# Gate tiles read and squared inside the projection loop, and buffers of their own for low parts, modulation and out tiles

## The chip, the cores and the metric

The kernel runs on one core of a Trainium2 chip. The metric is device time in microseconds: the median of the runs of one program. TensorE multiplies, VectorE and ScalarE do elementwise work, GpSimd (POOL) starts some DMAs and sums over partitions, SyncE (SP) starts most loads.

## The reference, cut to what matters

Two transformer layers over 256 tokens of width 2048, with a second stream of 256 context tokens. Layer 0 mixes by a Fourier transform, layer 1 by attention. The change lies in layer 0:

```python
shift, scale, gate = split(silu(c) @ ada_w[i] + ada_b[i], 3)      # modulation
h = rmsnorm(x, norm_g[i]) * (1 + scale) + shift
u, z = split(h @ w_in, 2)                                         # 4096 columns each
f = fft2(u, over tokens and in groups of 256).real                # 16 groups
f = einsum('bngc,gcd->bngd', f, w_mix)
y = f * silu(z)
x = x + gate * (y @ w_out[i])
```

The context stream goes through the same with its own modulation.

## The kernel before, in words

Every matmul in float32 is done as three cheaper ones, on a rounded high part and a low part of each operand (`mm3`: high by high, high by low, low by high). In the projection the parts are float32r (`split`: a ScalarE cast, line 66, then a VectorE subtraction, line 67). In the gate and out projections they are float16 with one scale for each weight tile. That scale comes from the tile's sum of squares: `squares` (a ScalarE activation, line 161, with a sum by row), `total` (line 165, POOL, over partitions), `scale` (VectorE, lines 170 and 171, and a ScalarE copy, line 173, where a second factor is folded in), and then `split16` (ScalarE line 179, VectorE line 180).

Layer 0 runs in these stages:

1. An opening: input loads, the first modulation vectors, the token transform.
2. The projection loop over 16 groups `g`. Each group loads two 1 MB weight halves `wu` into `rawp` (three buffers, tile name `raw`), folds them into m and p parts (line 134 and 140 on VectorE, or an accumulating DMA on POOL, line 143), splits them, and runs an m part and a p part of 48 matmuls each. `load_m` prepares a small matrix of the group (its cast is tile `mh`). `mix` multiplies the group before by its matrix and sends the result to DRAM (`fd`). `evacs[g]` are the cast and the subtraction that empty the p part of group g. The 16 tiles of gate columns 0 to 511 come as four shared tiles `wz0`; in groups 8 to 11 each is loaded into `raw` and squared there, for one common scale.
3. The gate loop. `make_hs` builds the 16 h tiles again in float16 (a load of xT by POOL, then VectorE line 768, ScalarE line 769, VectorE line 770). The four shared tiles are loaded again, split in halves, and multiplied into four outputs. Then come 28 private tiles `wz`, one for each output block b from 4 to 31, each 48 matmuls.
4. The out loop over 32 tiles `wo0` (n from 0 to 31).

`fetch(n)` loads tile n of stages 3 and 4, squares it and computes its scale; `weights(n)` splits it and calls `fetch(n + 2)`. `raw6` gives the tiles of wz, wo0 and adw in turn a buffer of `rawp` and one of `zp` (three each). `adw` are the 64 tiles of the remaining modulation weights: an `ada_step` takes one of them, and VectorE multiplies and reduces it with the condition rows in `cb` (line 730). Both halves of a split, high and low, come from `wsp` (six buffers).

The instructions of an engine run in a fixed order. That order is made when the program is built, by a planner that goes by the order of the program text and its own estimate of when operands are ready. `issue_after(x)` keeps the instructions of a block, on the engine of x, behind x; it adds no wait.

At the end of stage 4, `row_sums` adds squares by matmul for the next norm, and `x1_turn` transposes the stream for layer 1.

Of the kernel before, what the change touches and what calls it, by code (L numbers as in the profile page):

```python
# [32 lines left out]
def tile_dit(ctx: ExitStack, tc: tile.TileContext, a: dict, out: bass.AP):  # L33
# [21 lines left out]
    def act(dt=F32, n=512):  # L55
        return actp.tile([P, n], dt, tag="act", name="act")
# [512 lines left out]
        fill_pe(len(fill))  # L569


    w4 = adap.tile([P, 4], F32, name="w4")
    hsc = adap.tile([P, 2, KT, 2], F32, name="hsc")
    hq = [small("hq") for _ in range(3)]
    squares(hsc[:, 0], gs0, hq[0], 64.0)
    squares(hsc[:, 1], sh0, hq[1], 1.5)
    V.tensor_tensor(hq[2], hq[0], hq[1], op=ALU.add)
    hup, hdn = scale(total(hq[2]), None, "h", 1)
    V.tensor_scalar(hsc[:, 0], gs0, hup, None, op0=ALU.mult)
    V.tensor_scalar(hsc[:, 1], sh0, hup, None, op0=ALU.mult)  # L580
# [11 lines left out]
    for g in range(G):  # L592
# [33 lines left out]
            pqh, pql, sp = m1  # L626
        elif g > 2:
            pqh, pql, sp = load_m(g)
        if g == 13:
            w1 = small("w1", bufs=1)  # L630
            V.tensor_reduce(w1, w4, axis=AX.X, op=ALU.add)
            u4, d4 = scale(total(w1), hdn, "4", 1)
# [7 lines left out]
        if g > 3:  # L640
            with after_evac(g - 1), tc.issue_after(m_end[0]), tc.issue_after(m_end[1]):
                w[1]["p"] = split_part("p", v)
        oa = {} if g > 2 else ou[g]

        def part(xs, ks=range(KT)):
# [32 lines left out]
        pl = up.tile([127, 2, 130], F32R, tag="apl", name="apl")  # L678
        split(ph, pl, oa["p"])
        evacs.append((last_cast[0], last_sub[0]))  # L680

        def mix(g=g, mh=mh, ml=ml, ph=ph, pl=pl, pqh=pqh, pql=pql, sp=sp):
            for db in range(2):
# [32 lines left out]
    def ada_jobs():  # L716
        for pieces in ((0,), (1, 2, 3)):
            for kh in range(2):
                cb = adap.tile([P, 2, 1024], F32, tag="cb", name="cb")
                with tc.issue_after(hs_end[2]):  # L720
                    nc.gpsimd.dma_start(cb, a["crow"][:, kh].broadcast_to([P, 2, 1024]))
                with tc.issue_after(hs_end[1]):
                    S.activation(cb, cb, AF.Silu)  # L723
                for i in pieces:
                    for fg in range(8):
                        w = ada_raw(a["adw"][i, kh, fg])
                        for f in range(2):
                            wf = w[:, f * 1024 : f * 1024 + 1024]
                            for s in range(2 if i < 3 else 1):
                                V.tensor_tensor_reduce(junk, wf, cb[:, s], 1.0, 0.0, ALU.mult, ALU.add, acc[:, i, kh, fg * 2 + f, s : s + 1])  # L730
# [7 lines left out]


    adat = lay0.enter_context(tc.tile_pool(name="adat", bufs=1))  # L740
    junk = adat.tile([P, 1056], BF16, name="junk")[:, 0:1024]
    acc = adat.tile([P, 4, 2, KT, 2], F32, name="acc")
    YA = 8
    with tc.tile_pool(name="yp", reuse_waits="tile", bufs=33 - YA) as ypool, tc.tile_pool(name="zp", reuse_waits="tile", bufs=3) as zp:
        ys = [act() if b < YA else ypool.tile([P, 512], F32, tag="y", name="y") for b in range(NB)]
        hs = []
        hs_end = [None] * 3
        turn = [0]

        def raw6(src, view=lambda t, s: ((t, s),)):  # L750
            turn[0] += 1
            pool, nm = (rawp, "raw") if turn[0] % 2 else (zp, "rawz")
            t = pool.tile([P, D], F32, tag=nm, name=nm)
            for d, s in view(t, src):
                last_dma[0] = nc.sync.dma_start(d, s).ins
            return t

        ada_raw = raw6

        def make_hs(k):  # L760
            xt = act()
# [8 lines left out]
                hs_end[0] = V.scalar_tensor_tensor(l, t, hsc[:, 1, k, s : s + 1], h, op0=ALU.add, op1=ALU.subtract).ins  # L770
            hs.append((hl[:, 0:512], hl[:, 512:1024]))

        yq = adap.tile([P, NB], F32, name="yq")
        yup, ydn, yy = [None] * 2, [None] * 2, []

        def z_out(b, o, dn):
# [25 lines left out]
        def fetch(n):  # L802
            if n >= len(jobs):
                return
            nm, at_, i = jobs[n]
            if nm == "wz":
                t = raw6(a["wz"][at_])
            else:
                v = a["wo0"][at_[0] // 8, i * 8 : i * 8 + 8].rearrange("g p (j b f) -> p g j b f", j=2, b=8)[:, :, :, at_[0] % 8]
                t = raw6(v, lambda t, s: [(t.rearrange("p (g j f) -> p g j f", g=8, j=2)[:, :, j], s[:, :, j]) for j in range(2)])  # L810
            h, q = half16(), small("wq")
            squares(h, t, q)
            ready[n] = t, h, *scale(total(q), hdn if nm == "wz" else ydn[i])

        def weights(n):
            t, wh, up_, dn = ready.pop(n)
            wl = half16()
            split16(wh, wl, t, up_)
            fetch(n + 2)
            return wh, wl, dn  # L820

        o4 = [psum() for _ in range(4)]
        for kg in range(4):
            wr = raw6(a["wz0"][kg])
            wh, wl = half16(), half16()
            for i in range(2):
                make_hs(kg * 4 + i * 2)
                q = slice(i * 1024, (i + 1) * 1024)
                with tc.issue_after(hs_end[0]) if kg else nullcontext(), tc.issue_after(hs_end[1]) if kg else nullcontext():
                    split16(wh[:, q], wl[:, q], wr[:, q], u4)  # L830
                make_hs(kg * 4 + i * 2 + 1)
            for j in range(4):
                k = kg * 4 + j
                for b in range(4):
                    q = slice(j * 512 + b * P, j * 512 + (b + 1) * P)
                    mm3(o4[b], wh[:, q], wl[:, q], hs[k][0], hs[k][1], k == 0, k == KT - 1)
        for b in range(4):
            with tc.issue_after(last_dma[0]):
                nc.sync.dma_start(ys[b], fd[b])
        for b in range(4):  # L840
            z_out(b, o4[b], d4)
        fetch(0)
        fetch(1)
        for b in range(4, NB):
            wh, wl, dn = weights(b - 4)
            with tc.issue_after(last_dma[0]):
                nc.sync.dma_start(ys[b], fd[b])
# [12 lines left out]
        x1, sqs, xin = [], [], {}  # L860
        sq_end, st_end, sums = [None], [None], []

        def evac0(b, i, o, dn):
            t = xin[b]
            gd = adap.tile([P, 2], F32, tag="gd", name="gd", bufs=4)
            V.tensor_scalar(gd, gt0[:, b, :], dn, None, op0=ALU.mult)
            t2 = act() if i else None
            for s in range(2):
                q = slice(s * N, (s + 1) * N)
                V.scalar_tensor_tensor(t[:, q], o[:, q], gd[:, s : s + 1], t[:, q], op0=ALU.mult, op1=ALU.add)  # L870
                if i and b >= 14:
                    sq_end[0] = S.activation(t2[:, q], t[:, q], AF.Square).ins
# [16 lines left out]
        for n, (b, i) in enumerate(outs):  # L889
            if n == 0:  # L890
                y_scale(1)
            wh, wl, dn = weights(n + NB - 4)
            if n < 4:
                for _ in range(4):
# [21 lines left out]
    x1d = dram.tile([2, P, D], F32, name="x1d")  # L916
    gated = dram.tile([1, D], F32, name="gated")

    def x1_turn(tb, c):
# [4 lines left out]
        S.copy(t, o)  # L924
# [11 lines left out]
    with tc.issue_after(st_end[0]):  # L936
# [6 lines left out]
        for c, tb in ((0, 0), (0, 1), (1, 0), (1, 1), (2, 0)):  # L943
            x1_turn(tb, c)
    r_ps = [psum()[:, 0:N] for _ in range(2)]
    for t in range(4):
# [591 lines left out]
```

## Time and profile before

| what | value |
|---|---|
| median of 3 runs | 1791.06 us (1789.63 to 1796.57) |
| profiled execution, its own time | 1785.5 us |
| its span, first to last instruction | 1783.7 us |
| mean granted TensorE clock | 0.995 |
| projection, groups 8 to 15 | about 205 to 332 us |
| gate and out loops | about 333 to 1012 us |
| HBM read | 356.26 MB |

Rows of the profile name an engine, a line of the kernel, an operation and the tiles it writes and reads (`raw<-raw`). A number in brackets behind a row is the time for which the engine stood idle before it, with what ended that wait. A row of the waits has total microseconds, count and the longest.

### The profile page before, as it was taken

To read this page: it belongs to the slowest core of one execution; us is meant where nothing else is said; L and a number is where in the kernel's file an instruction comes from. 1 tells how busy PE (TensorE), PEld (TensorE's weight loads), DVE (VectorE), ACT (ScalarE), POOL (GpSimd) and SP (SyncE) were. 2 spreads that over 40 slices of the span, in tenths; PEclk is the share of its full clock that TensorE was granted. 3 is DMA by queue.
4 is the path that set the end of the run, shared out by engine and by line. 5 is a ranking of instruction groups with operands and counts; after the bars stand their busy time and mean duration, and the time that the engine had idled before them with its cause. 6 is when DMAs were issued, how large, how long until landed. Compare 5 with 4: busy or idle time off the path is not lost. (4 is left out here: it accounts for less than half of the span.)

```text
span 1783.7 us, 25965 instructions
## 1 busy us (share of the span) xinstructions
PE 1731.1 (97%) x9449; PEld 1204.6 (68%) x9449; DVE 1398.2 (78%) x2415; ACT 1039.3 (58%) x1708; POOL 256.6 (14%) x277
## 2 busy tenths in 40 slices
PE   6999999999999999999999999999999999999997
PEld 4679999644444444444444588788888888887886
DVE  5779778789889997953587463989999999997455
ACT  5544544485565656444334343777888888887343
POOL 0002111211000001100101000322212212234001
PEclk9999999999999999999999999999999999999999
DMA  9998898857777798654468323578898988888554
GB/s 393 417 340 230 234 279 237 288 214 283 275 261 264 259 327 256 204 164 130 131 226 275 112 97 104 174 179 219 213 208 211 216 208 208 210 216 262 197 179 142
DMA packets 267777, 403.06 MB, mean 226 GB/s; under 512 B 152641, under 2 KB 218577, under 8 KB 236161
## 3 DMA queue, kind: packets, MB, share of 16 engines
q1 hardware_dynamic: 243584, 363.39, 64.9%
q0 software_dynamic: 19920, 31.06, 6.9%
q10 hardware_dynamic: 4144, 6.95, 1.2%
q8 instruction: 74, 1.21, 0.3%
q14 instruction: 55, 0.44, 0.1%
HBM read 356.26 MB, written 12.59 MB: 207 GB/s over the span
## 5 line engine op out<-in xcount | busy, mean ns | idle before, releaser
L67 DVE TENSOR_TENSOR wl<-raw,wh 128x1024 fp32r<-128x1024 f32 x205 | 272.3, 1334 | 112.0 <-ACT wh L66 109.3
L66 ACT CAST wh<-raw 128x1024 fp32r<-128x1024 f32 x205 | 214.2, 1046 | 136.9 <-PE ps L80 123.6
L730 DVE CUSTOM_DVE_ANT_0 junk<-rawz,cb 128x1024 bf16<-128x1024 f32 x200 | 244.0, 1220 | 8.5 <-ACT cb L723 5.6
L80 PE MATMUL ps<-act,w 128*128 128x512 f16 x640 | 243.5, 381 | 0.5 <-DVE act L770 0.5
L79 PE MATMUL ps<-act,w 128*128 128x512 f16 x640 | 239.4, 381 | 4.0 <-ACT w L179 2.2
L81 PE MATMUL ps<-act,w 128*128 128x512 f16 x640 | 239.6, 379 | 0.2 <-DVE w L180 0.2
L1203 PE MATMUL ps<-h,wh 128*128 128x512 f32 x512 | 187.1, 403 | 0.0
L81 PEld LDWEIGHTS <-w 128*128 128x128 f16 x1024 | 100.2, 98 | 127.9 <-DVE w L180 6.8
L79 PEld LDWEIGHTS <-w 128*128 128x128 f16 x1024 | 100.4, 98 | 125.2 <-ACT w L179 3.3
L80 PEld LDWEIGHTS <-w 128*128 128x128 f16 x1024 | 100.4, 98 | 120.6 <-issue 0.8
L180 DVE SCALAR_TENSOR_TENSOR w<-raw,up,w 128x2048 f16<-128x2048 f32 (+1 forms) x58 | 131.8, 2274 | 51.5 <-PE ps L80 45.1
L161 ACT ACTIVATE w<-raw 128x2048 f16<-128x2048 f32 x54 | 102.8, 1904 | 94.2 <-PE ps L81 50.0
L81 PE MATMUL ps<-y,w 128*128 128x512 f16 x384 | 145.2, 379 | 4.0 <-DVE w L180 4.0
L80 PE MATMUL ps<-y,w 128*128 128x512 f16 x384 | 145.4, 379 | 0.0
L79 PE MATMUL ps<-y,w 128*128 128x512 f16 x384 | 144.9, 379 | 0.0
L1205 PE MATMUL ps<-h,wl 128*128 128x256 f32 x512 | 138.4, 281 | 0.0
L179 ACT ACTIVATE w<-raw,up 128x2048 f16<-128x2048 f32 (+1 forms) x58 | 112.1, 1935 | 23.3 <-DVE up L170 22.2
L80 PE MATMUL ps<-wl,h 128*128 128x512 f32 x320 | 125.1, 391 | 0.3 <-DVE wl L67 0.3
L81 PE MATMUL ps<-wh,h 128*128 128x512 f32 x320 | 123.8, 390 | 0.0
L79 PE MATMUL ps<-wh,h 128*128 128x512 f32 x320 | 122.4, 397 | 0.0
L165 POOL PARTITION_ALL_REDUCE tot<-wq x60 | 42.6, 713 | 541.5 <-ACT w L161 456.8
L1257 DVE SCALAR_TENSOR_TENSOR f<-p,sm,f 128x512 f16<-128x512 f32 x128 | 103.1, 824 | 12.0 <-ACT f L1256 11.8
(380 smaller groups left out, 4051.7 us busy)
## 6 DMA issues: line engine op xcount, KB each, us to landing
raw<-in_wz SPq DMA_DIRECT2D x65, 1024.0 KB, 5.3
rawz<-in_adw SPq DMA_DIRECT2D x56, 1024.0 KB, 5.1
raw<-in_awp SPq DMA_DIRECT2D x32, 1024.0 KB, 12.8
raw<-in_wq SPq DMA_DIRECT2D x32, 1024.0 KB, 5.2
raw<-in_wu SPq DMA_DIRECT2D x32, 1016.0 KB, 7.3
raw<-in_wo SPq DMA_DIRECT2D x54, 512.0 KB, 5.7
raw<-in_wo1b SPq DMA_DIRECT2D x16, 1024.0 KB, 4.9
act<-in_xT POOLq DMA_DIRECT2D x32, 256.0 KB, 6.3
```

Source lines behind the costliest of these rows:

```text
L66: last_cast[0] = S.copy(h, src).ins
L67: last_sub[0] = eng.tensor_tensor(l, src, h.bitcast(F32), op=ALU.subtract).ins
L79: PE.matmul(o, wh, xh, start=start, stop=False)
L80: PE.matmul(o, wh, xl, start=False, stop=False)
L81: return PE.matmul(o, wl, xh, start=False, stop=stop).ins
L161: sq_ins[0] = S.activation(dump, src, AF.Square, scale=scale, accum_out=col).ins
L179: last_cast[0] = S.activation(h, src, AF.Copy, scale=up).ins
L180: last_sub[0] = V.scalar_tensor_tensor(l, src, up, h, op0=ALU.mult, op1=ALU.subtract).ins
L730: V.tensor_tensor_reduce(junk, wf, cb[:, s], 1.0, 0.0, ALU.mult, ALU.add, acc[:, i, kh, fg * 2 + f, s : s + 1])
L1203: PE.matmul(o[0], wh[:, q], hx1[k], start=k == 0, stop=k == KT - 1)
L1205: PE.matmul(o[0][:, 0:N], wl[:, q], hx1[k][:, 0:N], start=False, stop=False)
L1257: V.scalar_tensor_tensor(f[:, 512:1024], pt[tb], sm[:, tb : tb + 1], f[:, 0:512], op0=ALU.mult, op1=ALU.subtract)
```

## The change

- The scale of the h tiles (`hsc`) is computed in groups 6 and 7 of the projection loop, not ahead of it.
- Six tiles, the four `wz0` and the first two `wz`, are read by `read_ahead` in groups 4, 6, ... 14 into the buffer `cb`, and squared there in two halves by `square_ahead` a group later. The scales of the first two private tiles are then known, and `fetch` only loads these.
- `adw` tiles have two `zp` buffers (`rawz`) to themselves; `wz` and `wo0` tiles use only the three of `raw`. Low parts have two buffers of their own (`wl`). One more y tile lies in the `act` pool (`YA`), one fewer in `yp`; `load_y` takes it when needed.
- The gate of layer 0 is multiplied by the scale of y once (`gty`), so `wo0` tiles need no ScalarE copy in `scale`.
- Steps of the modulation are dealt out otherwise: 31 instead of 28 in the gate loop, none in the first four tiles of the out loop, two at a time in tiles 5 to 8 and 25 to 28.
- Some orders are set anew (`wp_end`, `shared_end`), and one transposition goes ahead of the last row sums.

The diff, cut to its core:

```diff
+    def read_ahead(j):
+        src = a["wz0"][j] if j < 4 else a["wz"][j - 4]
+        ahead[0] = adap.tile([P, D], F32, tag="cb", name="cb")
+        nc.sync.dma_start(ahead[0], src)
+
+    def square_ahead(j):
+        for i in range(2):
+            t = ahead[0][:, i * 1024 : (i + 1) * 1024]
+            squares(t, t, w6[:, j * 2 + i : j * 2 + i + 1])
+
+    def scale_ahead(j, n, tag):
+        w1 = small("w1", bufs=3)
+        V.tensor_reduce(w1, w6[:, j * 2 : (j + n) * 2], axis=AX.X, op=ALU.add)
+        return total(w1), tag
...
-        if 8 <= g < 12:
-            t = raw(a["wz0"][g - 8])
-            squares(t, t, w4[:, g - 8 : g - 7])
...
+        if g in (4, 6, 8, 10, 12, 14):
+            with after_evac(g - 1):
+                read_ahead(g // 2 - 2)
+        elif g > 4:
+            with after_evac(g):
+                square_ahead(g // 2 - 2)
...
-        def raw6(src, view=lambda t, s: ((t, s),)):
-            turn[0] += 1
-            pool, nm = (rawp, "raw") if turn[0] % 2 else (zp, "rawz")
...
+        def ada_raw(src):
+            t = zp.tile([P, D], F32, tag="rawz", name="rawz", bufs=2)
+            nc.sync.dma_start(t, src)
+            return t
...
-            h, q = half16(), small("wq")
+            t = raw(a["wz"][at_]) if nm == "wz" else raw_wo(*at_)
+            h = half16()
+            if n < 2:
+                ready[n] = t, h, *first[n]
+                return
+            q = small("wq")
             squares(h, t, q)
-            ready[n] = t, h, *scale(total(q), hdn if nm == "wz" else ydn[i])
+            ready[n] = t, h, *scale(total(q), hdn if nm == "wz" else None)
...
-            wl = half16()
+            wl = zp.tile([P, D], F16, tag="wl", name="wl", bufs=2)
...
-            wr = raw6(a["wz0"][kg])
+            wr = raw(a["wz0"][kg])
...
-                with tc.issue_after(hs_end[0]) if kg else nullcontext(), tc.issue_after(hs_end[1]) if kg else nullcontext():
+                with tc.issue_after(hs_end[0] if kg else wp_end[1]), tc.issue_after(hs_end[1] if kg else wp_end[0]):
                     split16(wh[:, q], wl[:, q], wr[:, q], u4)
...
-            wh, wl, dn = weights(b - 4)
+            with tc.issue_after(shared_end[0]), tc.issue_after(shared_end[1]), tc.issue_after(hs_end[1]):
+                wh, wl, dn = weights(b - 4)
...
-                ada_step(1)
+                ada_step(2 if b in (7, 10, 13) else 1)
...
-            V.tensor_scalar(gd, gt0[:, b, :], dn, None, op0=ALU.mult)
+            V.tensor_scalar(gd, gty[i][:, b, :], dn, None, op0=ALU.mult)
...
-            ada_step(0 if n > 29 else 2 if n > 19 else 1)
+            ada_step(0 if n < 4 or n > 28 else 2 if 4 < n < 9 or n > 24 else 1)
...
-    row_sums(3)
+    with tc.issue_after(e), tc.issue_after(sq_end[0]):
+        x1_turn(0, 0)
+    with tc.issue_after(turn_end[0]):
+        row_sums(3)
```

More of the change, by code (lines that the diff above doesn't have):

```diff
@@ L569, in tile_dit @@
         fill_pe(len(fill))
-    w4 = adap.tile([P, 4], F32, name="w4")
+    w6 = adap.tile([P, 12], F32, name="w6")
     hsc = adap.tile([P, 2, KT, 2], F32, name="hsc")
[L574 to L580, printed above, removed]
+    ahead, early = [None], {}
+    def read_ahead(j):
[10 more added lines that the diff above has]
+        return total(w1), tag
     fd = [dram.tile([P, 512], F32, name=f"fd{b}") for b in range(NB)]
@@ L680, in tile_dit @@
         evacs.append((last_cast[0], last_sub[0]))
+        if g in (4, 6, 8, 10, 12, 14):
[4 more added lines that the diff above has]
+                square_ahead(g // 2 - 2)
+        if g in (6, 13, 15):
+            with after_evac(g):
+                if g == 6:
+                    hq = [small("hq") for _ in range(3)]
+                    squares(hsc[:, 0], gs0, hq[0], 64.0)
+                    squares(hsc[:, 1], sh0, hq[1], 1.5)
+                    V.tensor_tensor(hq[2], hq[0], hq[1], op=ALU.add)
+                    toth = total(hq[2])
+                else:
+                    early[g] = scale_ahead(*((0, 4, "4") if g == 13 else (4, 1, "5")))
+        if g in (7, 14):
+            with after_evac(g):
+                if g == 7:
+                    hup, hdn = scale(toth, None, "h", 1)
+                    V.tensor_scalar(hsc[:, 0], gs0, hup, None, op0=ALU.mult)
+                    V.tensor_scalar(hsc[:, 1], sh0, hup, None, op0=ALU.mult)
+                else:
+                    u4, d4 = scale(early[13][0], hdn, "4", 1)
         def mix(g=g, mh=mh, ml=ml, ph=ph, pl=pl, pqh=pqh, pql=pql, sp=sp):
@@ L740, in tile_dit, with load_y, raw_wo @@
     adat = lay0.enter_context(tc.tile_pool(name="adat", bufs=1))
-    junk = adat.tile([P, 1056], BF16, name="junk")[:, 0:1024]
+    junk = adat.tile([P, 1072], BF16, name="junk")[:, 0:1024]
     acc = adat.tile([P, 4, 2, KT, 2], F32, name="acc")
-    YA = 8
-    with tc.tile_pool(name="yp", reuse_waits="tile", bufs=33 - YA) as ypool, tc.tile_pool(name="zp", reuse_waits="tile", bufs=3) as zp:
-        ys = [act() if b < YA else ypool.tile([P, 512], F32, tag="y", name="y") for b in range(NB)]
+    YA = 9
+    with tc.tile_pool(name="yp", reuse_waits="tile", bufs=33 - YA) as ypool, tc.tile_pool(name="zp", reuse_waits="tile", bufs=2) as zp:
+        ys = []
+        def load_y(b):
+            ys.append(act() if b < YA else ypool.tile([P, 512], F32, tag="y", name="y"))
+            with tc.issue_after(last_dma[0]):
+                nc.sync.dma_start(ys[b], fd[b])
         hs = []
         hs_end = [None] * 3
-        turn = [0]
-        def raw6(src, view=lambda t, s: ((t, s),)):
-            turn[0] += 1
-            pool, nm = (rawp, "raw") if turn[0] % 2 else (zp, "rawz")
-            t = pool.tile([P, D], F32, tag=nm, name=nm)
-            for d, s in view(t, src):
-                last_dma[0] = nc.sync.dma_start(d, s).ins
-            return t
-        ada_raw = raw6
+        def raw_wo(b, i):
+            t = rawp.tile([P, D], F32, tag="raw", name="raw")
+            v = a["wo0"][b // 8, i * 8 : i * 8 + 8].rearrange("g p (j b f) -> p g j b f", j=2, b=8)
+            for j in range(2):
+                last_dma[0] = nc.sync.dma_start(t.rearrange("p (g j f) -> p g j f", g=8, j=2)[:, :, j], v[:, :, j, b % 8]).ins
+            return t
+        def ada_raw(src):
+            t = zp.tile([P, D], F32, tag="rawz", name="rawz", bufs=2)
+            nc.sync.dma_start(t, src)
+            return t
         def make_hs(k):
@@ L771, in make_hs @@
             hs.append((hl[:, 0:512], hl[:, 512:1024]))
-        yq = adap.tile([P, NB], F32, name="yq")
+        yq = adat.tile([P, NB], F32, name="yq")
+        gty = [adat.tile([P, KT, 2], F32, name=f"gty{i}") for i in range(2)]
         yup, ydn, yy = [None] * 2, [None] * 2, []
@@ L820, in weights @@
             return wh, wl, dn
+        first = [scale(early[15][0], hdn, "5", 1)]
+        first.append(scale(scale_ahead(5, 1, "6")[0], hdn, "6", 1))
         o4 = [psum() for _ in range(4)]
         for kg in range(4):
-            wr = raw6(a["wz0"][kg])
+            wr = raw(a["wz0"][kg])
             wh, wl = half16(), half16()
@@ L891, in tile_dit @@
                 y_scale(1)
+                for d, y in zip(gty, ydn):
+                    V.tensor_scalar(d, gt0, y, None, op0=ALU.mult)
             wh, wl, dn = weights(n + NB - 4)
```

26 lines of the change are left out of this document (9 added, 17 removed).

## The prediction

> **What bounds the kernel now.** I read the page first, then the waits of TensorE, then one window for each group of the projection loop.
>
> ```profile
> span 1783.7 us, 25965 instructions
> PE 1731.1 (97%) x9449; PEld 1204.6 (68%) x9449; DVE 1398.2 (78%) x2415; ACT 1039.3 (58%) x1708; POOL 256.6 (14%) x277
> ```
>
> TensorE is busy for 97% of the span, so 1783.7 - 1731.1 = 52.6 us is all that reordering can give back. The change leaves every matmul in place. The waits of TensorE say where that idle time lies:
>
> ```profile
> PE ps L79 <- DVE dh L214: 12.8, 2, 11.5
> PE ps L79 <- ACT mh L66: 7.9, 4, 3.7
> PE ps L81 <- DVE w L180: 4.2, 4, 1.5
> PE ps L79 <- ACT w L179: 2.2, 1, 2.2
> PE ps L79 <- ACT act L769: 1.6, 1, 1.6
> PE ps L885 <- ACT act L872: 1.0, 1, 1.0
> ```
>
> The columns are total us, times and longest. The first row is the start of the kernel, which the change doesn't touch. The others are its targets: the projection loop (mh), the out-projection loop (w L180), the handover between projection and gate (L179, L769) and the turn into layer 1 (L885).
>
> Next, the projection loop, cut where the last matmul of each group's p part ends, so that a window is a group (length, busy time and count by engine, clock, DMA share, GB/s):
>
> ```profile
> 191.30:205.75 14.45, 14.45 (x122) 14.45 (x122) 11.98 (x18) 8.88 (x15) 2.25 (x3) 1.00 0.91 239
> 205.75:220.20 14.45, 14.45 (x121) 14.24 (x119) 10.55 (x16) 6.53 (x10) 1.83 (x2) 1.00 0.65 245
> 220.20:236.02 15.82, 14.66 (x121) 14.45 (x120) 11.67 (x16) 6.58 (x16) 1.80 (x4) 1.00 0.94 282
> 236.02:255.97 19.95, 16.22 (x122) 16.22 (x123) 14.15 (x22) 11.17 (x18) 3.92 (x4) 0.91 0.81 236
> 255.97:270.44 14.47, 14.47 (x121) 14.25 (x119) 10.46 (x16) 6.25 (x13) 0.91 (x2) 1.00 0.94 290
> 270.44:287.25 16.81, 14.70 (x122) 14.70 (x123) 15.23 (x27) 9.35 (x17) 4.62 (x5) 1.00 0.77 213
> 287.25:301.73 14.48, 14.48 (x123) 14.48 (x122) 13.15 (x20) 7.30 (x15) 3.23 (x5) 1.00 0.92 246
> ```
>
> A group takes 14.45 to 14.48 us when TensorE never stops. Three take longer, by 1.36, 5.49 and 2.35 us: 9.2 us in all. In the worst one TensorE also lost clock (0.91). All three lie where the four shared gate tiles pass through the buffers of the projection's weights.
>
> **The change, part by part.**
>
> *Tiles read ahead in the projection loop.* Why those groups are long:
>
> ```profile
> 231.24 0.33 SPq L50 DMA_DIRECT2D raw<-in_wz  x1
> 238.27 5.09 SPq L50 DMA_DIRECT2D raw<-in_wu  x2
> 236.25 1.91 ACT L161 ACTIVATE raw<-raw 128x2048 f32<-128x2048 f32 x1 [0.68 <-DMA raw<-in_wz]
> 239.75 0.39 PE L79 MATMUL ps<-mh,ch 128*128 128x256 f32 x1 [3.73 <-ACT mh L66]
> L161 ACT ACTIVATE raw<-raw x4: 1906/1914/1923, 202.3 to 255.9; 128x2048 f32<-128x2048 f32 x4
> ```
>
> The square of a gate tile waited for its own load, and the cast of mh, which the next matmul needed, stood behind it on ScalarE. The tile also takes one of three weight buffers, so the next loads of wu go out late (238.27). After the change the tile goes to the idle cb buffer a whole group before its square, and the square stands behind the evacuation of the p part. Neither cause is left. The squares grow: six tiles in two halves. The half has no row; the nearest is the cast of 128x1024, 1046 ns (the page's L66 row below), so 6 x 2 x 1.05 = 12.6 us against 4 x 1.91 = 7.6. In every second group that is 2.1 us more on an engine that is busy for 6.2 to 8.9 of 14.45 us: hidden, unless a cast queued behind it is late, which then costs at most those 2.1 us a group.
>
> ```profile
> L66 ACT CAST wh<-raw 128x1024 fp32r<-128x1024 f32 x205 | 214.2, 1046 | 136.9 <-PE ps L80 123.6
> 45.00:90.00 45.00, 43.18 (x339) 30.10 (x337) 31.91 (x68) 23.32 (x41) 0.00 (x0) 1.00 1.01 417
> ```
>
> The reads themselves: a quiet group moves 239 x 14.45 = 3.5 MB, two groups with one read 7.0 + 1.05 = 8.0 MB. At the loop's best rate, 290 GB/s, that is 27.8 us of 28.9, so it fits, barely. (The Trainium skill, "DMA: Bandwidth & Descriptors", section Specifications, gives about 358 GB/s as one core's limit of HBM; by that the two groups would take 22.5 us, and the reads would be free with room to spare. The trace bears out neither side of that figure here: the opening reached 417, the loop with its small packets never passed 290.) The bounds for this part are a gain of 9.2 us (no group loses anything) and a loss of 4.6 us (six reads lose what four lost: 9.2 / 4 x 6 = 13.8). I take 8.0, near the gain, because its two causes are seen in the rows and both go.
>
> *The h scales and totals* move from ahead of the loop into it: a few instructions of 32 columns or fewer and three more reductions on POOL (14% busy). Hidden by matmuls; 0, within 0.3 either way.
>
> *Handover.* Rows of TensorE's other waits there, and ScalarE and the load queue in order of time:
>
> ```profile
> PE ps L79 <- ACT mh L66: 1.1, 1, 1.1
> PE ps L80 <- DVE act L770: 0.5, 1, 0.5
> 308.34 16.20 SPq L755 DMA_DIRECT2D raw<-in_wz  x4
> 336.93 11.56 SPq L755 DMA_DIRECT2D rawz<-in_wz  x3
> 340.67 0.91 ACT L769 ACTIVATE act<-act,hsc 128x256 f16<-128x256 f32 x2 [0.95 <-DVE act L768]
> 345.66 1.15 ACT L179 ACTIVATE w<-rawz,up 128x1024 f16<-128x1024 f32 x1 [4.08 <-DMA rawz<-in_wz]
> 351.22 1.13 ACT L179 ACTIVATE w<-rawz,up 128x1024 f16<-128x1024 f32 x1
> 356.77 1.14 ACT L179 ACTIVATE w<-raw,up 128x1024 f16<-128x1024 f32 x1
> 368.90 1.90 ACT L161 ACTIVATE w<-raw 128x2048 f16<-128x2048 f32 x1
> 370.80 1.89 ACT L161 ACTIVATE w<-rawz 128x2048 f16<-128x2048 f32 x1
> 372.69 0.89 ACT L769 ACTIVATE act<-act,hsc 128x256 f16<-128x256 f32 x2
> ```
>
> Waits here: 2.2 + 1.6 + 1.1 + 0.5 = 5.4 us. The second shared tile waited in the queue for a rawz buffer, issued at 336.93, and its split for the landing (345.66). After the change it comes through raw, whose buffers took loads from 308.34 to 324.54, so the split can follow the cast of the h tile before it (make_hs, L769) at 340.67 + 0.91 = 341.6. The sixth tile's square may stand there first (2.1 us): 341.6 to 343.7. The two squares at 368.90 and 370.80, 3.8 us ahead of an h tile that TensorE waited for (372.69), are gone. What is late next is the chain of h tiles: two of them with half a split take 356.77 - 351.22 = 5.55 us, and TensorE's 24 matmuls on two of them less: a private tile's 48 take 496.31 - 485.99 = 10.3 us (rows below), so 5.2. And the first private tile, which filled TensorE's gap before, is now split only behind the last h tile. So I count 2.5 of the 5.4, near the middle of the 2.0 to 4.1 us by which the split moves up, less a little for the pace; the ends are 5.4 and a loss of 2.35, if the first private split (L180, 2.35 us) stands wholly in the open.
>
> *Low parts of their own, three raw buffers for wz and wo, two for adw.*
>
> ```profile
> 951.00 1.91 ACT L161 ACTIVATE w<-raw 128x2048 f16<-128x2048 f32 x1 [7.96 <-DMA raw<-in_wo]
> 734.72 2.35 DVE L180 SCALAR_TENSOR_TENSOR w<-raw,up,w 128x2048 f16<-128x2048 f32 x1
> 485.99 2.35 DVE L180 SCALAR_TENSOR_TENSOR w<-raw,up,w 128x2048 f16<-128x2048 f32 x1
> 496.31 2.35 DVE L180 SCALAR_TENSOR_TENSOR w<-raw,up,w 128x2048 f16<-128x2048 f32 x1
> 400.00:650.00 250.00, 250.00 (x1161) 113.33 (x1159) 235.24 (x374) 145.65 (x188) 20.14 (x27) 1.00 0.75 271
> SPq L755 <- DVE acc L730: 174.8, 45, 7.7
> ```
>
> The gate loop (400 to 650) has no idle TensorE; nothing to gain there. The out loop has 4.2 us in four waits for the split. Late ones come from out tiles that land late, because adw takes turns in the same six buffers (951.00), from reductions put ahead of a split in the first four out tiles (734.72), which get no step now, and from scale copies between. I take 3.0 of 4.2; 0 and 4.2 are the ends, and the loss is a rival. The 32 copies of the scale that go are ScalarE work that hides anyway. A low part now has two buffers, so a split starts when the tile before last is done, one tile of 10.3 us ahead of need, and takes 2.35; VectorE has 250 - 235.24 = 15 us idle in 24 tiles, and the reductions are filler that can run ahead. 0.
>
> *Turn into layer 1.* One group of transposes fills the 1.0 us wait for the last squares, but the same sums still end the chain: 0, at most 1.0. One more y tile in act, gd from gty, other pools: no instruction on the path.
>
> Sum: 8.0 + 2.5 + 3.0 = 13.5 us. The profiled execution took 1785.5 us, so 1772.0; the three runs have their median 5.6 above it (1791.06), so I forecast 1791.06 - 13.5 = 1777.5.
>
> **Rivals.**
>
> 1. *The loads stay the bound of the loop.* For it: the DMA share is 0.91 to 0.94 in most groups, and the pair has 1.1 us to spare. Against it: quiet groups move their weights with no wait of TensorE. Then six reads cost 13.8: 4.6 more than now, less 2.5 and 3.0: 1790. (The Trainium skill, the same page, section "Issuing engines are not separate DMA queues", says that all queues end on the same 16 engines; by that alone another buffer gives no bandwidth, and this would be the case. The group at 290 GB/s, which kept its pace, speaks against it.)
> 2. *Only the loop gains.* The h tiles pace the handover, and new splits are as late as the old in the out loop: 1791.06 - 8.0 = 1783.
> 3. *Slower: the load queue.* SyncE issues in order. Already 45 adw loads held it, 174.8 / 45 = 3.9 us each, until reductions freed a buffer. With two buffers instead of a share in six, a doubled step puts two such waits ahead of the next weight tile. There are 11 doubled steps; if each costs TensorE 3.9 us, 43 - 13.5 gives 1820. It decides from six such stalls on (22.5 us); against it, weight loads go out more than a tile ahead.
>
> **How the numbers follow.** About 0.5% (9 us) is what a measurement of this kernel can tell from no change. The forecast, a gain of 9 to 20 us (1771 to 1782), gets 0.60; rival 1 0.15; rival 2 0.15; rival 3 0.10. So faster 0.60, same 0.30, slower 0.10. The range runs from all the gains (9.2 + 5.4 + 4.2 + 1.0 = 19.8, so 1771, and 1.4 lower, as the fastest run before lies under its median) to rival 1 with nothing gained at the handover: 1770 to 1792.
>
> **What would show it.** Groups at 14.45 us from the fourth to the fifteenth, and no square waiting for a load, prove the first part; groups of 16 us with a late wu prove rival 1. The wait for w L179 at the handover should be gone, and one for L769 left. No wait for w L180 in the out loop proves the third; waits of SyncE for the reductions with TensorE idle behind them, rival 3. It would be wrong above all if the squares, in their new place, delayed a cast that TensorE needs in every second group.

## The result, and the profile after

The changed kernel is slower: 1812.48 us median of 6 runs (1809.10 to 1816.68) against 1791.88 us of the kernel before (1785.58 to 1796.57), ratio 1.0119 [1.0095, 1.0143]. The forecast was 1777.5 (1770 to 1792). The medians lie 20.6 us apart, but the two traces 31.2: the profiled execution after is the longest of the six (1816.68), and the one before is as short as the shortest (1785.5). So the traces make the loss some 10 us larger than the medians do.

The page after:

```profile
span 1814.9 us, 25926 instructions
PE 1741.7 (96%) x9449; PEld 1203.3 (66%) x9449; DVE 1402.6 (77%) x2419; ACT 1035.4 (57%) x1688; POOL 248.4 (14%) x277
```

TensorE's waits after, over the whole span (us in total, times, longest):

```profile
PE ps L81 <- DVE wl L180: 30.4, 22, 3.3
...
PE ps L246 <- DMA raw<-in_awp: 4.1, 3, 3.4
...
PE ps L79 <- ACT y L179: 1.3, 1, 1.3
PE ps L79 <- ACT mh L66: 1.1, 1, 1.1
```

The targets in the projection loop and at the handover are hit: mh fell from 7.9 to 1.1 us, and the handover's waits for L179 and L769 are gone (the L179 row left is the start of the out loop). One row grew more than all of them shrank: the wait for the low part of a weight tile, 4.2 us in 4 before, is 30.4 us in 22 (`wl` is the low part's tile, `w` its name before).

The stages (us, from the starts of the 16-bit matmuls in the traces; 192 of them work on shared gate tiles, 1344 on private ones, 1536 on out tiles):

| kernel | to first 16-bit matmul | shared tiles | 28 gate tiles | 32 out tiles | rest | end |
|---|---|---|---|---|---|---|
| before | 332.9 | 49.4 | 290.1 | 339.3 | 771.9 | 1783.7 |
| after | 326.2 | 42.7 | 299.7 | 370.8 | 775.4 | 1814.9 |

So 13.4 us were gained as far as the gate tiles, 9.6 lost in them, 31.5 in the out tiles and 3.5 in the rest: 31.2 us. The gain first. The projection loop of the changed kernel, one window for each group, in the columns of the prediction (length; busy and count of PE, PEld, DVE, ACT, POOL; clock; DMA share; GB/s):

```profile
195.25:209.73 14.48, 14.48 (x123) 14.48 (x122) 13.11 (x20) 7.59 (x17) 3.49 (x5) 1.00 0.94 244
209.73:224.21 14.48, 14.48 (x122) 14.48 (x122) 13.03 (x22) 9.04 (x17) 2.61 (x3) 1.00 1.07 323
...
238.68:253.16 14.48, 14.48 (x123) 14.48 (x122) 12.78 (x18) 8.93 (x17) 2.60 (x3) 1.00 1.10 332
...
sum 101.34, PE 101.34 PEld 101.34 DVE 89.36 ACT 56.07 POOL 19.05; mean PE 14.48 PEld 14.48 DVE 12.77 ACT 8.01 POOL 2.72
```

TensorE never stops, and the three of these seven groups that have a read move 312 to 332 GB/s. The same seven groups took 301.73 - 191.30 = 110.43 us before. Then the loss, in four windows:

```profile
400.00:650.00 250.00, 245.75 (x1135) 110.23 (x1134) 215.35 (x336) 137.04 (x176) 11.11 (x25) 1.00 0.68 245
650.00:735.00 85.00, 76.25 (x334) 33.01 (x333) 55.74 (x95) 44.46 (x49) 7.25 (x14) 0.96 0.71 235
735.00:945.00 210.00, 199.82 (x906) 88.56 (x905) 166.41 (x291) 81.55 (x67) 15.86 (x27) 0.98 0.67 213
945.00:1040.00 95.00, 85.11 (x396) 38.90 (x394) 28.02 (x47) 23.75 (x23) 5.34 (x12) 0.98 0.34 101
```

In the last window TensorE loses 10 of 95 us although VectorE, which it waits for, works for only 28.0, ScalarE for 23.8, and the DMA share is 0.34. VectorE, ScalarE and the DMA have time to spare there: it is a chain. The trace of that window in order of time, VectorE, ScalarE, POOL and the load queue (a number in brackets: idle before, and what ended it):

```profile
950.93 2.34 DVE L180 SCALAR_TENSOR_TENSOR wl<-raw,up,w 128x2048 f16<-128x2048 f32 x1
953.30 25.55 SPq L786 DMA_DIRECT2D raw<-in_wo  x6
959.83 1.91 ACT L161 ACTIVATE w<-raw 128x2048 f16<-128x2048 f32 x1 [7.17 <-DMA raw<-in_wo]
961.65 0.19 ACT L161 ACTIVATION_READ_ACCUMULATOR w<-raw 128x1 f32 x1
961.94 0.38 POOL L165 PARTITION_ALL_REDUCE tot<-wq  x1 [11.64 <-ACT w L161]
962.35 0.15 DVE L170 TENSOR_SCALAR up<-tot 128x1 int32<-128x1 int32 x1 [8.34 <-POOL tot L165]
962.61 0.88 DVE L907 SCALAR_TENSOR_TENSOR act<-ps,gd,act 128x256 f32<-128x256 f32 x2
963.41 2.34 DVE L180 SCALAR_TENSOR_TENSOR wl<-raw,up,w 128x2048 f16<-128x2048 f32 x1
```

Number the 60 tiles of the gate and out loops n = 0 to 59 as `fetch` does. The split of n = 53 ends at 953.27 and so frees its weight buffer; the load of n = 56 goes out at 953.30; its square starts at 959.83, its sum over partitions is there at 962.32, VectorE takes the scale of n = 56 at 962.35, then an evacuation, and only then the split of n = 54, which ends at 965.75. The split of 54 needs nothing of tile 56: its own operands were long there. It stands behind the scale of 56 in VectorE's order. So each split here waits for a load that the split before it released. One turn, from split to split, is the split, the load, the square, the total, and the scale with the evacuation: 2.34 + 6.56 + 2.11 + 0.41 + 1.06 = 12.48 us (11.83 the time before), where TensorE needs 10.36 for a tile's 48 matmuls. VectorE's own waits show the same. After, from 690 to 1040 us:

```profile
DVE up L170 <- POOL tot L165: 81.9, 24, 8.5
```

Before, from 690 to 1012 us:

```profile
DVE w L180 <- PE ps L80: 40.6, 10, 4.6
...
DVE up L170 <- POOL tot L165: 14.8, 8, 2.8
```

There it was mostly the split that waited, for a buffer, ahead of need. In the order before, the scale of n + 1 and not of n + 2 stood ahead of the split of n, so that the same chain had two tiles' time. VectorE before, the split of n = 56, the scale of 58 and the split of 57:

```profile
964.14 2.33 DVE L180 SCALAR_TENSOR_TENSOR w<-raw,up,w 128x2048 f16<-128x2048 f32 x1
...
973.33 0.15 DVE L170 TENSOR_SCALAR up<-tot 128x1 int32<-128x1 int32 x1 [2.18 <-POOL tot L165]
...
975.94 2.34 DVE L180 SCALAR_TENSOR_TENSOR w<-rawz,up,w 128x2048 f16<-128x2048 f32 x1
```

Counted over both traces, the scale of n + 2 stands ahead of the split of n in none of the tiles before, and in 38 of the 60 after.

### The profile page after: what moved, and what is told of

The parts are those of the page before. It is cut to its first block, busy times and chain, and to the rows that moved or that the text cites. A ratio compares the mean times of both kernels' runs of the same rounds, so it can differ in the third digit from the quotient of the medians.

```text
span 1814.9 us, 25926 instructions
## 1 busy us (share of the span) xinstructions
PE 1741.7 (96%) x9449; PEld 1203.3 (66%) x9449; DVE 1402.6 (77%) x2419; ACT 1035.4 (57%) x1688; POOL 248.4 (14%) x277
## 5 line engine op out<-in xcount | busy, mean ns | idle before, releaser
L758 DVE CUSTOM_DVE_ANT_0 junk<-rawz,cb 128x1024 bf16<-128x1024 f32 x224 | 273.4, 1220 | 22.6 <-DMA rawz<-in_adw 12.9
L81 PE MATMUL ps<-act,wl 128*128 128x512 f16 x592 | 228.2, 385 | 26.7 <-DVE wl L180 26.0
L80 PE MATMUL ps<-act,w 128*128 128x512 f16 x656 | 251.7, 384 | 0.0
L79 PE MATMUL ps<-act,w 128*128 128x512 f16 x656 | 249.2, 384 | 0.0
L81 PEld LDWEIGHTS <-wl 128*128 128x128 f16 x960 | 94.5, 98 | 156.8 <-DVE wl L180 43.4
L80 PEld LDWEIGHTS <-w 128*128 128x128 f16 x1024 | 100.9, 99 | 122.8 <-issue 4.3
L79 PEld LDWEIGHTS <-w 128*128 128x128 f16 x1024 | 100.9, 99 | 120.9 <-issue 5.0
L179 ACT ACTIVATE w<-raw,up 128x2048 f16<-128x2048 f32 (+1 forms) x68 | 128.9, 1899 | 41.8 <-DVE up L170 41.4
L81 PE MATMUL ps<-y,wl 128*128 128x512 f16 x368 | 139.4, 379 | 4.4 <-DVE wl L180 4.4
L180 DVE SCALAR_TENSOR_TENSOR wl<-raw,up,w 128x2048 f16<-128x2048 f32 x60 | 140.6, 2343 | 3.6 <-ACT w L179 2.9
L79 PE MATMUL ps<-y,w 128*128 128x512 f16 x368 | 138.9, 379 | 1.3 <-ACT y L179 1.3
L80 PE MATMUL ps<-y,w 128*128 128x512 f16 x368 | 139.3, 379 | 0.5 <-DVE y L180 0.4
L1288 ACT ACTIVATE p<-ps,mx 128x512 f32<-128x512 f32 x128 | 87.8, 688 | 39.6 <-DVE mx L1285 32.9
```

Of the source, the lines that this page charges most:

```text
L79: PE.matmul(o, wh, xh, start=start, stop=False)
L80: PE.matmul(o, wh, xl, start=False, stop=False)
L81: return PE.matmul(o, wl, xh, start=False, stop=stop).ins
L179: last_cast[0] = S.activation(h, src, AF.Copy, scale=up).ins
L180: last_sub[0] = V.scalar_tensor_tensor(l, src, up, h, op0=ALU.mult, op1=ALU.subtract).ins
```

## The experiments

All start from the changed kernel unless said otherwise. Each ratio is against runs of the kernel before on the same chip. "Good" below is the order with the scale of n + 1 ahead of the split of n, "bad" the one with n + 2; "depth" is the number of buffers for low parts.

| kernel | median us | ratio to before | 28 gate tiles | 32 out tiles |
|---|---|---|---|---|
| changed kernel | 1812.48 | 1.0119 [1.0095, 1.0143] | 299.7 | 370.8 |
| order mended | 1780.30 | 0.9958 [0.9945, 0.9972] | 290.1 | 346.3 |
| low parts in the shared buffers | 1771.32 | 0.9900 [0.9886, 0.9913] | 290.1 | 334.6 |
| steps of before | 1803.82 | 1.0083 [1.0069, 1.0096] | 294.7 | 366.6 |
| before, with own low parts | 1837.48 | 1.0273 [1.0259, 1.0288] | 296.3 | 378.3 |
| half squares | 1820.48 | 1.0161 [1.0138, 1.0183] | 298.5 | 381.3 |
| quarter squares | 1810.41 | 1.0105 [1.0087, 1.0124] | 303.0 | 365.6 |
| three low parts | 1770.11 | 0.9884 [0.9865, 0.9903] | 290.1 | 334.3 |
| three low parts, order forced bad | 1792.42 | 1.0017 [1.0006, 1.0028] | 290.1 | 357.5 |
| the same, out tiles' squares halved | 1768.91 | 0.9904 [0.9888, 0.9921] | 290.1 | 334.8 |
| shared low parts, first read later | 1764.96 | 0.9848 [0.9828, 0.9869] | 290.1 | 338.0 |
| three low parts, first read later | 1764.86 | 0.9863 [0.9843, 0.9884] | 290.1 | 334.3 |

**The order mended, nothing else.**

```diff
             split16(wh, wl, t, up_)
-            fetch(n + 2)
+            with tc.issue_after(last_sub[0]):
+                fetch(n + 2)
```

(`last_sub` is VectorE's part of the split of n; the guard keeps the scale of n + 2 behind it.)

> The changed kernel with one thing else: tile n+2 (load, square, scale) may not be issued on the engines before the subtraction of tile n's split, so that VectorE's order has the scale of n+2 behind the split of n and not ahead of it. Two own low-part buffers, doubled reduction steps and read-ahead stay. Theory (a cycle: split n-1 frees the weight buffer, load n+2 6 us, square 2.1, total 0.4, scale of n+2, evacuation 0.9, only then split n 2.3: 12 us for a tile of 10.36): the wait for the low part in the out loop falls from 30.4 us to under 6, the gate loop gets back some 5 us, and the time is 1775 to 1785. Rival 'two low-part buffers are too few by themselves': the split still waits for TensorE's end of the tile before last, time 1805 to 1815. Rival 'SyncE's queue': adw loads still hold weight loads back, 1805 to 1815.

32 us less, as the theory had it. VectorE at the same place of this kernel:

```profile
961.19 0.88 DVE L908 SCALAR_TENSOR_TENSOR act<-ps,gd,act 128x256 f32<-128x256 f32 x2 [6.33 <-PE ps L81]
961.98 2.34 DVE L180 SCALAR_TENSOR_TENSOR wl<-raw,up,w 128x2048 f16<-128x2048 f32 x1
964.61 0.15 DVE L170 TENSOR_SCALAR up<-tot 128x1 int32<-128x1 int32 x1 [0.28 <-POOL tot L165]
```

The split, of n = 57, starts 9.4 us before its tile does, paced by TensorE (the evacuation waits for its tile), and the scale's wait is 0.28 in place of 8.34 us. With two low parts the order alone takes 24.5 of the 36.2 us by which the out tiles of the changed kernel exceed those of the next run. 11.7 us stay: TensorE still waits at n = 32 (1.0 and 2.2 us, for the split of y) and at n = 49 and 51 (1.9 us each, on the matmul that reads the low part). These weren't followed further, so a smaller cost of the depth itself stays open.

**Low parts in the shared buffers** (`wl = half16()`), adw buffers and doubled steps as in the change.

> The changed kernel with the low parts again in the six shared 4 KB buffers (three low parts deep); adw buffers, doubled steps, read-ahead stay. Theory: a split has no longer to wait in the plan for the tile before last, so the order has the split of n ahead of the scale of n+2: wait for the low part under 6 us in the out loop, 1770 to 1782. Rival 'two low-part buffers themselves': the same gain, so this run alone doesn't tell them apart. Rival 'SyncE's queue of adw loads': still 1805 to 1815, since the adw loads have the same two buffers.

1771.3, and in its trace no row of TensorE's waits for a low part of a weight tile is left at all. It keeps the three weight buffers of the change, so these alone don't make the loss. The load queue speaks against the rival. SyncE's waits for reductions from 690 to 1040 us, in the changed kernel:

```profile
SPq L791 <- DVE acc L758: 44.1, 12, 7.0
```

And in this one, which loses nothing by them:

```profile
SPq L791 <- DVE acc L758: 43.7, 10, 5.2
```

**The reduction steps of before.**

```diff
-                ada_step(2 if b in (7, 10, 13) else 1)
+                ada_step(1)
...
-            ada_step(0 if n < 4 or n > 28 else 2 if 4 < n < 9 or n > 24 else 1)
+            ada_step(0 if n > 29 else 2 if n > 19 else 1)
```

> The changed kernel with the reduction steps of before (one a tile, two from the 21st out tile), all its buffers kept. Theory: the order has the scale of n+2 ahead of the split of n in most out tiles still, 1803 to 1815. Rival 'SyncE's queue' (the eleven doubled steps hold weight loads back): 1780 to 1790.

As the theory had it, 1803.8: the doubled steps are not the cause of most of the loss. The 8.7 us between are less waiting in both loops; this run doesn't say whether fewer reductions or the other order that they leave did it.

**Before, with low parts of their own** (`wl` from two `zp` buffers as in the diff of the change, `bufs=3` of `zp` cut to 2). One part of the change alone, on the other kernel.

> The kernel before, with only this: low parts in two buffers of their own, and the second set of weight buffers cut from three to two to make room. No read-ahead, no doubled steps. Theory: the order has the scale of n+2 ahead of the split of n in about ten out tiles (38 to 47 of all 60) at 1.5 us each or more, so slower than before by 8 to 25 us: 1800 to 1817. Rival 'read-ahead, doubled steps or the moved y scaling did it': about 1791.

1837.5, worse than the theory's 1800 to 1817, and without any of the gains: out tiles 39.0 us longer than before, gate tiles 6.2, shared tiles 5.6. TensorE's wait for the low part and VectorE's for the total, over 320 to 1045 and 690 to 1040 us:

```profile
PE ps L81 <- DVE wl L180: 33.4, 23, 4.4
DVE up L170 <- POOL tot L165: 95.8, 25, 9.9
```

The same signature, without read-ahead and without the new steps: the scale of n + 2 stands ahead of the split of n in 38 tiles here too. So low parts of their own suffice for a loss of this kind. The edit also leaves one weight buffer fewer; what that costs wasn't run by itself.

**Half and quarter squares.** The chain has the square in it, so a shorter square should shorten the loss.

```diff
-            squares(h, t, q)
+            squares(h[:, 0:1024], t[:, 0:1024], q, 1.5)
```

> The changed kernel, but the sum of squares of each later weight tile is taken over half of its columns (1024 of 2048, scaled), which leaves out half of that sum; VectorE's order keeps the scale of n+2 ahead of the split of n in all out tiles. Theory (the cycle has the square of 1.91 us in it): a tile's turn falls from 11.9 to about 10.9 us against TensorE's 10.36, so the out loop loses 0.5 a tile and not 1.5: time 1788 to 1800, wait for the low part 10 to 18 us in place of 30.4. Rival 'order or buffers cost by themselves, not by the length of the chain' (ScalarE isn't busy): stays 1805 to 1815.

> The same with a quarter of the columns (512, scaled): the turn is about 10.4 us, TensorE's own pace. Theory: wait for the low part under 6 us, time 1777 to 1788 with the order as bad as in the changed kernel. Rival 'order or buffers cost by themselves': 1805 to 1815.

Both times missed their forecasts (1788 to 1800, 1777 to 1788), and the second lies in the range of the rival, though near the end of the out loop the turn did what the theory says. VectorE with half squares, first near the end of the out loop, then where reductions still run:

```profile
963.55 2.34 DVE L180 SCALAR_TENSOR_TENSOR wl<-raw,up,w 128x2048 f16<-128x2048 f32 x1
974.55 2.35 DVE L180 SCALAR_TENSOR_TENSOR wl<-raw,up,w 128x2048 f16<-128x2048 f32 x1
...
878.62 0.15 DVE L170 TENSOR_SCALAR up<-tot 128x1 int32<-128x1 int32 x1 [2.06 <-POOL tot L165]
878.69 1.22 DVE L758 CUSTOM_DVE_ANT_0 junk<-rawz,cb 128x1024 bf16<-128x1024 f32 x1
...
879.95 1.23 DVE L758 CUSTOM_DVE_ANT_0 junk<-rawz,cb 128x1024 bf16<-128x1024 f32 x1
...
881.89 2.34 DVE L180 SCALAR_TENSOR_TENSOR wl<-raw,up,w 128x2048 f16<-128x2048 f32 x1
```

At the end a turn is 974.55 - 963.55 = 11.0 us (12.0 on average in the changed kernel, from the split of n = 53 to that of n = 57). But the expectation took the order of the changed kernel to be bad in all out tiles, and it was so in 17 of 32 (every second one from n = 40 to 50). The planner, told of a shorter square, made it 26, and in many of those one or two reductions of 1.2 us stand between scale and split, inside the turn. What was won by the square was lost again. The edit moved two things, so these two runs don't decide.

**Three low parts.** Every third low part from a shared buffer, so the depth is three and the squares stay free to run early.

```diff
-            wl = zp.tile([P, D], F16, tag="wl", name="wl", bufs=2)
+            wl = half16() if n % 3 == 0 else zp.tile([P, D], F16, tag="wl", name="wl", bufs=2)
```

> The changed kernel with every third low part in a shared 4 KB buffer, so that low parts are three deep while the squares are as free as in the change. Theory: with three low parts the order has the scale of n+1, and not of n+2, ahead of the split of n in nearly all out tiles, so the cycle is two tiles long: wait for the low part under 6 us, 1771 to 1782. Rival 'what makes the order bad is that squares are free to run early, not the depth of the low parts': 1800 or more.

1770.1, with no wait for a low part. With three the planner puts the scale of n + 2 ahead of the split in one tile only, with two in 38. What in its estimate does this wasn't looked at.

**Three low parts, and the bad order by force.** Depth and order are now apart: the order mended was depth two with a good order, this is depth three with a bad one.

```diff
+            if n >= 32:
+                fetch(n + 2)
+            with tc.issue_after(up_end[0]) if 32 <= n < 58 else nullcontext():
-            split16(wh, wl, t, up_)
-            fetch(n + 2)
+                split16(wh, wl, t, up_)
+            if n < 32:
+                fetch(n + 2)
```

(`up_end` is the scale of the tile fetched last.)

> The version with three low parts (every third in a shared buffer), and in 26 out tiles the split of n may be issued on VectorE only behind the scale of n+2, as the changed kernel's order had it. Buffers three deep, order bad. Theory: a turn is split 2.34, load 5.9, square with its read-out 2.1, total 0.4, scale 0.2, together 11.0 us (the evacuation lies ahead of the scale here, so it isn't in the turn), 0.6 us or more over TensorE's 10.36 in 26 tiles: 1784 to 1800, a wait for the low part of 12 us or more in the out loop. Rival 'it is the depth of the low parts': 1769 to 1773, no wait.

1792.4: 22 us slower by the order, with the same buffers. VectorE's turns (`w` is the low part from a shared buffer), 11.2 us from split to split:

```profile
947.00 0.15 DVE L170 TENSOR_SCALAR up<-tot 128x1 int32<-128x1 int32 x1
947.07 2.34 DVE L180 SCALAR_TENSOR_TENSOR w<-raw,up,w 128x2048 f16<-128x2048 f32 x1
...
958.19 0.15 DVE L170 TENSOR_SCALAR up<-tot 128x1 int32<-128x1 int32 x1 [7.67 <-POOL tot L165]
958.27 2.35 DVE L180 SCALAR_TENSOR_TENSOR wl<-raw,up,w 128x2048 f16<-128x2048 f32 x1
```

And TensorE's waits for low parts, from 325 to 1045 us, 14.5 us where the same buffers with the planner's order have none:

```profile
PE ps L81 <- DVE w L180: 8.4, 5, 3.2
PE ps L81 <- DVE wl L180: 6.1, 7, 1.5
```

**The same, with the out tiles' squares halved.** Now the order is held, so that only the length of the turn changes.

> The version with three low parts and the order forced bad (scale of n+2 right ahead of the split of n in 26 out tiles), and the sum of squares of the out tiles from n = 32 of 60 on taken over half of their columns, which leaves out half of that sum. The order is held this time. Theory: the square's 1.91 us becomes about 1.0, the turn 10.9 becomes 10.0, under TensorE's 10.36: the out loop's waits go but for the one of the first bad tile (3 us), and the time falls from 1792 to 1768 to 1776. Rival 'a bad order costs by itself, whatever the length of the turn': 1788 to 1796.

1768.9, within what the theory gave; the rival had 1788 to 1796. No wait for a low part is left from 325 to 1045 us, and two splits 945.22 - 934.75 = 10.47 us apart keep TensorE's pace with the scale of n + 2 still right ahead of each:

```profile
934.67 0.15 DVE L170 TENSOR_SCALAR up<-tot 128x1 int32<-128x1 int32 x1 [5.90 <-POOL tot L165]
934.75 2.35 DVE L180 SCALAR_TENSOR_TENSOR wl<-raw,up,w 128x2048 f16<-128x2048 f32 x1
...
945.11 0.15 DVE L170 TENSOR_SCALAR up<-tot 128x1 int32<-128x1 int32 x1 [6.90 <-POOL tot L165]
945.22 2.35 DVE L180 SCALAR_TENSOR_TENSOR wl<-raw,up,w 128x2048 f16<-128x2048 f32 x1
```

So with turns no longer than a tile the bad order costs next to nothing: 334.8 us of out tiles against 334.3 with the good one.

**The first read later.** The changed kernel's opening lost 3.0 us: the last matmul of line 246 starts at 118.5 in place of 115.5 us, and the longest wait there for raw<-in_awp is 3.4 in place of 0.8 us. Its load queue shows why:

```profile
13.37 0.33 SPq L579 DMA_DIRECT2D cb<-in_wz  x1
```

The first read-ahead, written for group 4 of the projection, went out 13 us after the start, between the loads of the opening: cb was free, and `after_evac` names instructions of ScalarE and VectorE, which hold back nothing on SyncE.

```diff
-            with after_evac(g - 1):
+            with after_evac(g - 1), tc.issue_after(last_dma[0]):
                 read_ahead(g // 2 - 2)
```

> The version with the low parts in the shared buffers, and the first of the six read-ahead loads may be issued only behind the load of the fifth step's frequency weights on SyncE (in the changed kernel it went out 13.4 us after the start, between the loads that the opening waits for). Theory: the opening's wait for raw<-in_awp falls from 3.1 to about 0.8, the first 16-bit matmul from 325.8 to about 323.3, and the time from 1771.3 to 1767 to 1770. Rival 'the opening's loss isn't that load' or 'the load only delays others later': 1771 to 1773, first 16-bit matmul at 325 or later.

> The version with three low parts, and the first read-ahead load behind the fifth step's frequency weights. Theory: both gains add: 2.4 us in the opening, and the out loop without the one wait of 3.7 us (tile 33 of 60) that the version with shared low parts had: 1760 to 1768, no wait for a low part. Rival: the two gains are one and the same slack: 1765 to 1771.

TensorE's waits in the first of the two:

```profile
PE ps L246 <- DMA raw<-in_awp: 1.4, 5, 0.4
```

It takes 1764.96, below the forecast's 1767 to 1770, with the first 16-bit matmul at 322.2 us in place of 325.7 without the edit. The second adds both edits in its trace (out tiles 334.3 in place of 338.0, last 16-bit matmul at 989.2 in place of 992.9), but its median is the same; the 3.7 us that the out loop gains don't show in the time. The waits that the first has and the second lacks, 3.2 us in all, lie at n = 32 and are for the split of y, not for a low part. Both are faster than either kernel of this case, by 1.4 to 1.5% against before.

## Why the prediction was wrong

1. *Tiles read ahead:* right. Seven groups gave 110.43 - 101.34 = 9.1 us, just under the upper bound of 9.2; 8.0 was forecast. Groups take 14.48 us and no square waits for its load, as the test asked. Rival 1 falls: groups with a read moved up to 332 GB/s, more than the 290 that the prediction took for the loop's best. Not counted: the read that went out in the opening and cost 3.0 us there; the prediction took the start of the kernel as untouched.
2. *Handover:* right in kind, too small. The shared tiles fell by 49.4 - 42.7 = 6.7 us, where 2.5 was taken and 5.4 was the end. The first split of the second shared tile moved from 345.66 to 331.85 (row below), where 341.6 to 343.7 was forecast, and no wait for an h tile (L769 before) was left, where the test expected one. Two h tiles with half a split still take 5.55 us against TensorE's 5.2, as forecast, but the splits never fall behind: they start 6.0 us ahead of the matmuls that read them at the second tile and 3.7 at the last.

```profile
331.85 1.13 ACT L179 ACTIVATE w<-raw,up 128x1024 f16<-128x1024 f32 x1
```

3. *Low parts of their own: 0.* This is the step that failed. It reads: "a split starts when the tile before last is done, one tile of 10.3 us ahead of need". That is when its buffer is free, not when its turn comes on VectorE. The sentence asked for VectorE's throughput (15 us idle in 24 tiles) and never for what would stand ahead of the split in the fixed order, nor how long the chain behind that is. The rows of that chain were there to be added: split 2.35 and square 1.91 in the prediction's own fences; with 6.5 us from a load's issue to its square (measured here, after) they give 10.8 us, more than 10.3, before the total and an evacuation. With the good order the sentence comes out (the order mended), in the changed kernel the turn of 12.0 us does not fit. It cost 9.6 + 31.5 us of the trace; low parts in the shared buffers alone take 41.2 us off the median.
4. *Out loop: 3.0.* The gain is there where the order is good: with low parts shared or three deep, the out tiles take 334.3 to 334.6 us, 4.7 to 5.0 less than before, even above the upper bound of 4.2 (338.0 in the run that waits for y). No run tells apart the three reasons that the prediction gave for it. In the changed kernel step 3 buried it. Rival 2 (only the loop gains) falls with this and with the handover's 6.7 us.
5. *Turn into layer 1: 0.* The wait for the last squares fell from 1.0 to 0.6 us, but the time shows no sign of it: the rest takes 771.1 to 776.5 us in the eleven kernels that have the change's code there, and before lies in that spread with 771.9.
6. *Rival 3* had the sign and a place near by, but not the cause: it laid the wait on adw loads in SyncE's queue. SyncE waits for the low part's split, which frees the weight buffer (184.9 us in 26 waits from 690 to 1040 us), and its waits for reductions are as long in a kernel that loses nothing. Its price of eleven doubled steps also left out that the kernel before has eight (n = 20 to 27 of the out loop).

With step 3 and the early load mended, the trace of the version with shared low parts gains 10.7 + 6.7 + 1.3 - 1.7 = 17.0 us by stages (13.5 forecast). Its median lies 27 us under that of before: single executions of one kernel lie up to 11 us apart, and the two profiled ones are a short one of before and the longest of this.

The Trainium skill says in "Perfetto Trace Analysis", section "Optimization Strategy", that a gap which repeats over a stretch can mean that there isn't memory enough for the next tile (buffer count, tile sizes). Here the trace agrees only half way: the gap repeats and a third buffer removes it, but so, for the most part, does the order alone with two (1780.3), and three buffers with the bad order keep it (1792.4).

## What to carry to other kernels

In a loop whose engines have a fixed order, write down the ring "buffer free, load, what is computed of the load, what stands ahead of the release on that engine" and compare its length with the time that the slowest engine needs for one tile; idle engines don't help a ring. A change of buffer counts also changes what the planner puts first, so look at the new order around each instruction that frees a buffer. A guard on order holds only the engine that it names: a load on another queue may go out at once.

## What the runs showed of the hardware

A long wait costs TensorE more than itself. Windows of two neighbouring tiles near the end of the changed kernel, and TensorE in order of time behind the second one's wait:

```profile
999.59:1011.33 11.74, 10.54 (x50) 4.62 (x49) 2.87 (x3) 2.17 (x3) 0.88 (x2) 1.00 0.54 185
1011.33:1026.29 14.96, 12.21 (x49) 5.01 (x48) 6.63 (x9) 0.81 (x2) 0.00 (x0) 0.89 0.41 142
```

```profile
1014.67 0.39 PE L81 MATMUL ps<-act,wl 128*128 128x512 f16 x1 [2.75 <-DVE wl L180]
1015.36 0.63 PE L81 MATMUL ps<-act,wl 128*128 128x512 f16 x1
...
1018.74 0.38 PE L80 MATMUL ps<-act,w 128*128 128x512 f16 x1
```

The second tile waited 2.75 us, and for the 3.4 us from 1015.36 to 1018.74 its matmuls start 0.43 us apart in place of 0.22 (granted clock 0.89 over the tile): 1.7 us more. Five of the 60 tiles in this trace have 7 or 8 such slow starts, each time behind a gap between matmul starts of 2.57 us or more; single gaps up to 2.32 us slowed none here. Over the experiments gaps of 2.4 to 3.8 us went either way (2.46 us slowed them in one run, 3.77 did not in the same), and all but one of those over 3 us slowed the matmuls. The Trainium skill, "TensorE: Matmul & The Clock Gate", section "Part 1: The HAM clock gate (the 'warmup' mystery)", gives half rate after an idle window of about 3.4 us, and full rate after a busy one; the slow stretch agrees (3.4 us), while waits shorter than the window already set it off here.
